# A decoder step whose instruction order is planned at build time: the plan's delays between engines raised, its 40 random rounds replaced by 1405 recorded steps

## The chip, the cores and the metric

The kernel runs on one core of one Trainium2 chip. The metric is the device time of one execution in microseconds, as the median of several runs. The profile is of one further execution.

The engines are TensorE (PE, matmuls; its weight loads are shown as PEld), VectorE (DVE), ScalarE (ACT), GpSimd (POOL) and SyncE (SP), which issues the DMAs. Each works through its own queue in the order in which its instructions were written, and waits on semaphores for what other engines have to deliver.

## The reference

One inference step of a two-layer decoder on 512 prompt tokens and 8 sequences of 8 sample tokens, all in float32, model width 1024:

```python
for i in range(DEPTH):                       # 2 layers
    h = rms_norm(x, norm_mix_pre[i])
    m = pool_mixer(h, ...) if i % 2 == 0 else gdn_mixer(h, ...)
    x = x + rms_norm(m, norm_mix_post[i])
    h = rms_norm(x, norm_ffn_pre[i])
    x = x + rms_norm(swiglu(h, ffn_w_in[i], ffn_w_out[i]), norm_ffn_post[i])
```

The pooling mixer takes trailing means over 2, 4, 8 and 16 positions and a small product per group of channels. The gated DeltaNet mixer projects to q, k, v, z and gates, runs a short causal convolution, normalizes q and k, and runs a chunked delta rule over 16 heads (a triangular inverse per chunk, then a recurrence over chunks that carries a state). A gate and an output product follow. Each SwiGLU FFN has an inner width of 2816. Outputs are the new tokens and all new states.

## The kernel before, in words

**Tiling.** The 576 tokens stand in the free dimension, in two halves of 256 and 320 columns (`HALVES`); channels stand in the 128 partitions. Products in float32 are made of three products of split operands: `mm3` (in `hybrid_kernel`) multiplies high by high, high by low and low by high parts. A weight tile is loaded as `wraw` (three buffers), rounded to `wh` on ACT, and the rest `wl` is made on DVE or POOL (`Weights.split`). The FFNs use a scheme with seven products in place of eight (`seven`). Results stand in eight PSUM banks, handed out in rings by `bank`: three for half one (`ps_A`), three for half two (`ps_B`), two for the mixer's projections (`ps_m`), two for the delta rule (`ps_k`), others for transposes (`ps_x`), the scan (`ps_s`) and norms (`ps_n`).

**Stages.** First the pooling mixer, then the FFN of layer 0, then the DeltaNet mixer in four groups of four heads, then the FFN of layer 1. In the mixer, `core` makes the delta rule of one group (`inv32`, `sample_front`, `scan`, `sample_heads`), `project` the projections of the next, `zproj` the z heads (`ps_m`, then Silu into `zz`, then out to memory), and `out0` the first half of the output product, kept in `y_d`. After the mixer its memory pools are closed; `yo` takes over their place, is loaded from `y_d`, and the second half of the output product is added to it.

**What sets the order.** The function does not issue instructions. Each call on an engine is recorded by `Plan.put` (reached through `Plan.Engine`) as an operation with its predecessors, its cost on each engine that may do it (`Plan.cost`: how long it holds the engine and when it is done), and the PSUM tiles it uses. There are 15384 such operations. `Plan.finish` then sets the order of all five queues:

- It gives each operation a rank, the length of the longest path from it to the end.
- `forward(rank)` plays the program through by the costs. At each moment, it takes the engine that is free first and gives it, of the operations that have become available, the one of the highest rank. An operation becomes available at the end of its last predecessor plus `LAT` of its own engine (between two PE operations, as soon as PE is free). Where PE would wait more than 300 ns, `idle_until` puts idle matmuls of `ones` into an unused bank (`ps_w`), which keep PE active. The model also follows PE's clock (`WINDOW`, `LOAD`) and the DMA queue. `forward` returns the order, the times and the whole length.
- `backward(order, times)` plays a given order from the end and returns the latest time for each operation; its negative is a new rank.
- In 40 rounds, the rank from `backward` is disturbed (`stirred`: all operations that write the same tile get the same random offset of up to 0, 300, 1000 or 3000 ns), `forward` is played again, and the shortest order is kept.

The order found is then issued, one instruction after the other (line 300; the idle matmuls on line 296).

Of the kernel before, what the change touches and what calls it, by code (L numbers as in the profile page):

```python
# [4 lines left out]

# [45 lines left out]
ZB = (0, 4, 8, 10, 12, 16)  # L51


class Plan:


# [208 lines left out]
    def finish(self):  # L267
        self.on = False
        ops = self.ops
        n = len(ops)  # L270
# [4 lines left out]
        rank = [0.0] * n
        for i in range(n - 1, -1, -1):
            e = ops[i][7]
            hold, done = ops[i][1][e]
# [4 lines left out]
            rank[i] = r
        draw = random.Random(self.SEED)
        here = best = self.forward(rank)
        for _ in range(self.ROUNDS):
# [4 lines left out]
            if found[0] < best[0]:
                best = found
        with self.tc.manual_schedule():
            for i, e in best[1]:
                if e is None:
                    self.tc.nc.tensor.matmul(self.banks[i[0]][i[1]][0][:, :self.idle.shape[1]], self.idle, self.idle,  # L296
                                             start=True, stop=True)
# [2 lines left out]
                calls[e](*a, **k)  # L300

    def stirred(self, rank, stir, draw):

        if not stir:
            return rank
        off = {}
        for o in self.ops:
            off.setdefault(self.name(o), stir * (2.0 * draw.random() - 1.0))
        return [r + off[self.name(o)] for r, o in zip(rank, self.ops)]
# [506 lines left out]

# [1131 lines left out]
```

## Time and profile before

| | us |
|---|---|
| median of 3 runs | 1572.15 (1570.51 to 1574.17) |
| the profiled execution | 1572.64 |
| its span, first to last instruction | 1570.9 |
| matmuls | 11962 |
| mean granted TensorE clock | 0.991 |
| bytes moved by DMA | 198.92 MB, mean 127 GB/s |

The profile gives, for each engine, the time in which it was busy, and, for each idle time, which instruction on which engine ended it. Nearly every instruction has line 300, the line that issues the plan, so groups are told apart by the names of their tiles: `ps_m<-hH,wh` is a matmul into a tile `ps_m` of the tiles `hH` and `wh`. Busy time by stretch, and of one tile alone, shows where in the kernel time is lost. The idle matmuls `ps_w` count as busy.

### The profile page before, as it was taken

How to read it: one execution, taken by the hardware profiler on the slowest of the kernel's cores; microseconds unless marked ns; L12 is line 12 of the kernel's file. 1: busy time of each engine (PE TensorE's matmuls, PEld its weight loads, DVE VectorE, ACT ScalarE, POOL GpSimd, SP SyncE). 2: the span in 40 equal slices, each digit the busy share in tenths (PEclk: the TensorE clock that was granted, in tenths of full speed). 3: DMA queues.
4: the chain of work that ended last, by engine and by line, in shares of the span. 5: the costliest groups of instructions: out<-in, count | busy, mean ns of one | idle time of the engine just before them, and what ended most of it. 6: DMA issues, size and time to landing. Idle time of an engine off the chain costs nothing. (4 is left out here: it accounts for less than half of the span.)

```text
span 1570.9 us, 30641 instructions
## 1 busy us (share of the span) xinstructions
PE 1542.9 (98%) x11962; PEld 1481.2 (94%) x11962; DVE 1154.5 (73%) x2333; ACT 841.1 (54%) x1756; POOL 113.1 (7%) x258
## 2 busy tenths in 40 slices
...
GB/s 184 103 178 142 82 94 95 96 80 91 151 210 158 83 119 117 102 123 100 136 109 108 106 127 120 201 140 179 248 173 177 107 81 73 88 110 68 98 187 119
DMA packets 350359, 198.92 MB, mean 127 GB/s; under 512 B 13963, under 2 KB 344364, under 8 KB 350207
## 3 DMA queue, kind: packets, MB, share of 16 engines
...
## 5 line engine op out<-in xcount | busy, mean ns | idle before, releaser
L300 ACT ACTIVATE wh<-wraw 128x1024 fp32r<-128x1024 f32 (+1 forms) x227 | 233.5, 1032 | 263.2 <-PE ps_B L300 94.4
L300 DVE TENSOR_TENSOR wl<-wraw,wh 128x1024 fp32r<-128x1024 f32 (+2 forms) x226 | 268.0, 1191 | 113.6 <-ACT wh L300 74.9
L300 PE MATMUL ps_m<-hH,wh 128*128 128x320 f32 (+1 forms) x832 | 244.1, 310 | 2.7 <-ACT zz L300 2.6
L300 PE MATMUL ps_m<-hL,wh 128*128 128x320 f32 (+1 forms) x832 | 242.4, 306 | 0.0
L300 PE MATMUL ps_m<-hH,wl 128*128 128x320 f32 (+1 forms) x832 | 239.2, 306 | 0.0
L300 PEld LDWEIGHTS ps_m<-hH,wh 128*128 128x128 f32 x832 | 153.3, 189 | 7.6 <-ACT zz L300 3.6
L300 PEld LDWEIGHTS ps_m<-hL,wh 128*128 128x128 f32 x832 | 154.0, 190 | 2.3 <-issue 0.6
L300 PEld LDWEIGHTS ps_m<-hH,wl 128*128 128x128 f32 x832 | 152.6, 190 | 2.8 <-issue 0.8
L300 PE MATMUL ps_B<-hH,wh 128*128 128x320 f32 (+1 forms) x392 | 115.8, 306 | 0.2
L300 PE MATMUL ps_B<-hH,wl 128*128 128x320 f32 (+1 forms) x392 | 115.0, 305 | 0.0
L300 PE MATMUL ps_B<-hL,wh 128*128 128x320 f32 (+1 forms) x392 | 114.6, 304 | 0.0
L300 PE MATMUL ps_A<-hH,wh 128*128 128x256 f32 (+1 forms) x376 | 106.0, 293 | 2.8 <-DVE yo L300 1.9
L300 PE MATMUL ps_A<-hH,wl 128*128 128x256 f32 (+1 forms) x376 | 105.6, 292 | 0.5 <-DVE wl L300 0.5
L300 PE MATMUL ps_A<-hL,wh 128*128 128x256 f32 (+1 forms) x376 | 104.5, 290 | 0.1
L300 PE MATMUL ps_B<-aH,wl 128*128 128x320 f32 x352 | 103.5, 312 | 0.2 <-DVE wl L300 0.2
L300 PE MATMUL ps_B<-aH,wh 128*128 128x320 f32 x352 | 102.4, 311 | 0.0
L300 PE MATMUL ps_B<-aL,wh 128*128 128x320 f32 x352 | 101.9, 310 | 0.0
L300 PE MATMUL ps_A<-aH,wh 128*128 128x256 f32 x352 | 95.1, 283 | 0.4 <-ACT wh L300 0.4
L300 PE MATMUL ps_A<-aL,wh 128*128 128x256 f32 x352 | 94.0, 281 | 0.0
L300 PE MATMUL ps_A<-aH,wl 128*128 128x256 f32 x352 | 92.9, 282 | 0.0
L300 DVE SCALAR_TENSOR_TENSOR ac<-u,cwt,ac 128x600 f32<-128x600 f32 x96 | 80.9, 850 | 1.9 <-ACT ac L300 1.7
L300 ACT ACTIVATE aH<-sg 128x576 fp32r<-128x576 f32 (+2 forms) x56 | 32.3, 581 | 84.7 <-DVE sg L300 84.7
...
## 6 DMA issues: line engine op xcount, KB each, us to landing
...
```

What stands on the lines that cost most here:

```text
L300: calls[e](*a, **k)
```

## The change

Only `Plan` is edited; the operations that are recorded stay the same.

1. The table of delays between engines, `LAT`, in ns by the engine that receives: PE from 55 to 190, ACT from 36 to 120, DVE from 36 to 120, POOL from 70 to 150; SP stays at 60.
2. The 40 random rounds go. In their place stand 1405 recorded moves, each a field "again.seed.stir.lo.hi" in base 36. For each move: if `again` is set (10 of them), the rank is replaced by the negative latest times of its own order; if `stir` is set (100, 300, 1000 or 3000 ns), the operations from `lo` to `hi` in the list get an offset of up to that size, from a hash of the seed and of the first operation that writes the same tile. Half of the moves span 400 operations or fewer. Moves lie in all parts of the list, most densely in its last quarter.
3. One last `forward` gives the order.

```diff
+MOVES = """
+1.1d7anak.0.rf.u7 1.y2f47l.2s.0.bvc 1.s0vq82.2s.0.ti 1.pp743b.0.0.bvc 1.4z4ke2.0.9qg.a1k 0.au7bb7.2s.7t9.bo5
...
-    LAT = {"PE": 55.0, "ACT": 36.0, "DVE": 36.0, "POOL": 70.0, "SP": 60.0}
+    LAT = {"PE": 190.0, "ACT": 120.0, "DVE": 120.0, "POOL": 150.0, "SP": 60.0}
...
-    ROUNDS, STIR, SEED = 40, (0.0, 0.0, 300.0, 1000.0, 3000.0), 2
...
-        draw = random.Random(self.SEED)
-        here = best = self.forward(rank)
-        for _ in range(self.ROUNDS):
-            late = self.backward(here[1], here[2])
-            found = self.forward(self.stirred([-t for t in late], draw.choice(self.STIR), draw))
-            if found[0] < here[0] or draw.random() < 0.1:
-                here = found
-            if found[0] < best[0]:
-                best = found
+        first = {}
+        of = [first.setdefault(self.name(o), i) for i, o in enumerate(ops)]
+        for move in MOVES.split():
+            again, seed, stir, lo, hi = (int(x, 36) for x in move.split("."))
+            if again:
+                rank = [-t for t in self.backward(*self.forward(rank)[1:])]
+            if stir:
+                for i in range(lo, hi):
+                    rank[i] += stir * self.noise(seed, of[i])
+        best = self.forward(rank)
...
+    @staticmethod
+    def noise(seed, who):
+
+        h = seed ^ (who * 2654435761 & 0xffffffff)
+        h ^= h >> 16
+        h = h * 0x85ebca6b & 0xffffffff
+        h ^= h >> 13
+        h = h * 0xc2b2ae35 & 0xffffffff
+        h ^= h >> 16
+        return h / 2147483648.0 - 1.0
```

More of the change, by code (lines that the diff above doesn't have):

```diff
@@ L2 @@
 import heapq
-import random
 from contextlib import ExitStack
@@ new lines @@
+0.xfacbh.2s.781.8dp 0.1fp5dk3.2bc.3ok.3zo 0.1slwoeh.2bc.70z.86n 0.1vgjcmy.2s.82h.985 0.1gi4m9f.2bc.4hm.4ke
+0.87h1q0.rs.54h.5fl 0.rfnq0w.8c.8ql.bvc 0.q4hmzs.8c.9sc.a3g 0.10nufsc.2s.0.1q5 0.1tiapdn.2s.b6l.bvc
+0.17t45od.rs.4a9.855 0.5rdedg.rs.9tc.9w4 0.1j4zh0k.2bc.6e.96 0.1ss67k0.rs.a6f.ahj 0.2svvgn.8c.agj.ajb
+0.bpoomp.rs.bpu.bsm 0.t3o181.2bc.41f.4cj 0.1wv9twd.2s.1ck.57g 0.1tf1mpa.8c.od.1u1 0.69rvzm.2bc.9fe.9qi
+0.1pj35r4.rs.9r8.9u0 0.1ce0uqr.8c.2um.40a 0.gjfyk0.8c.0.6p 0.46rblf.2s.3gc.3rg 0.14ty5f3.2s.8u9.9zx
@@ new lines @@
+0.g581av.8c.3cf.4i3 0.mnk81z.8c.8o2.8z6 0.qqg7s0.8c.8u9.9zx 0.1umehv5.8c.69r.6cj 0.163iv7o.8c.9zj.a2b
+0.1u5svau.rs.aa7.alb 0.gwwnl4.rs.3xw.490 0.8mc1r3.8c.6by.6eq 0.19w15z5.rs.9y7.a0z 0.ttisib.2bc.0.2w
+0.a7ikvn.2s.6mv.6pn 0.1bygjfd.2s.bnt.bvc 0.1koaur1.rs.8pn.90r 0.1wf7dro.rs.98t.9jx 0.ji5ev1.rs.a90.ak4
+0.1yp3jqj.rs.bfn.bif 0.1jv2yn6.rs.5vg.5y8 0.1mws14w.8c.8bp.9hd 0.i1evgw.2s.4gk.4jc 0.e2qeak.2bc.bb5.bm9
+0.11gd8un.rs.92n.95f 0.1favvlm.8c.1fj.1ib 1.3ktxmq.0.7cu.7fm 0.177ynii.rs.9pq.ave 0.1r5eqxe.8c.33t.3ex
@@ new lines @@
+0.ma35m2.rs.1d5.2it 0.lymuvx.8c.2td.34h 0.1x8yzja.2s.a8.454 0.muxcdo.8c.8sl.8vd 0.14uzngk.2s.5gn.6mb
+0.n0a1h5.8c.3t.3yp 0.1vmszuc.2s.36d.3hh 0.1kk9pm2.rs.7dk.7oo 0.17owqc0.2s.b0l.bvc 0.1cw9cxp.2bc.9n4.9y8
+0.elx6d7.8c.5in.6ob 0.1dkpzq2.2bc.86x.89p 0.9mpa4v.8c.5dp.5ot 0.jijbp0.2bc.b6h.bhl 0.x120r.2s.7cw.8ik
+0.2qokrq.rs.9ax.agl 0.ap74jx.rs.50w.5c0 0.1qf2ph5.rs.7w9.7z1 0.w56vte.rs.7ba.7e2 0.msgyjb.rs.6yq.84e
+0.psozk2.2bc.8p9.8s1 0.6ru0ma.2bc.aag.alk 0.1ilo347.2s.8nn.bvc 0.yqg8b1.2s.a62.a8u 0.1mz5fg.8c.9ek.ak8
@@ new lines @@
+0.7ta4rs.8c.5i9.5td 0.1a0iey2.rs.9wh.b25 0.m5lp1v.2s.38j.3jn 0.zowpr1.rs.241.2f5 0.18btd35.rs.9ha.amy
+0.67gkgs.8c.7lg.7wk 0.j1z5x4.2bc.98j.9jn 0.1p7860q.rs.91j.a77 0.1pz1vr6.rs.8mg.9s4 0.1fipxct.rs.973.9i7
+0.abp70g.rs.80m.8bq 0.15geaz8.2s.mv.pn 0.8n6wmv.rs.b8j.bvc 0.arqvcn.rs.1yx.21p 0.1osivhj.8c.3bg.3mk
+1.nd1zyp.rs.4lg.8gc 0.17z6qfn.2s.0.3g0 0.1renpzd.8c.9ja.aoy 0.10phdap.8c.81y.8d2 0.1s3qh7q.2bc.74c.774
+0.15e6smx.8c.1nb.2sz 0.1y1qmao.rs.5yz.61r 0.1qrour4.2s.0.31t 0.kdlkj4.2s.98f.9jj 0.du8s9v.8c.32y.3e2
@@ new lines @@
+0.zod3gs.rs.b1b.b43 0.kr24fj.rs.85t.8gx 0.jcsbb1.2s.7h9.8mx 0.1x13xnh.8c.1iq.1li 0.1ph2m2d.8c.jd.m5
+0.1obr04.2s.1bk.2h8 0.v8xpgw.2s.8ca.8f2 0.j1t9fl.8c.3g3.3r7 0.lmds8a.2s.bf2.bhu 0.mhzsom.2s.bhf.bvc
+0.g1j1ok.2s.893.9er 0.1ahwx7x.rs.80f.837 0.tj5xya.8c.akf.bq3 0.4n5glo.rs.9d2.9o6 0.15a5n8l.2s.7kq.7vu
+0.al1vf1.rs.97d.9ih 0.37vrb0.2bc.bfi.bia 0.30028l.2s.3wy.482 0.1t59vpp.8c.9ec.9h4 0.dlech0.2s.88d.8b5
+0.1v4x5fz.8c.6lg.7r4 0.1mwug70.rs.a1i.a4a 0.1ynuagv.2s.59y.5l2 0.12049ht.2bc.615.63x 0.t1q1ic.rs.9fy.alm
@@ new lines @@
+0.fxf9yv.rs.9eu.aki 0.1mgx6i9.2bc.55l.58d 0.vcvc52.8c.8zz.92r 0.19sl7ib.8c.7li.7wm 0.r0plbe.rs.asc.b3g
+0.7zanmx.rs.b05.bvc 0.12ufhff.8c.9jy.apm 0.4avjfd.8c.awb.b7f 0.hns5r3.rs.20o.23g 0.la7cq1.2s.9a9.afx
+0.7yxen0.2s.3xw.490 0.v5sum0.rs.arg.bvc 0.120epcx.2s.a48.afc 0.8u617z.8c.bu2.bvc 0.wteemh.8c.8am.8de
+0.wq6dw1.8c.b20.b4s 0.ez6f38.2s.bu1.bvc 0.12rv7la.2s.aob.btz 0.1ldfvg7.2s.bjn.bvc 0.169st4w.2s.3fz.4ln
+0.rvl2k.2s.88j.9e7 0.105hv1b.2s.jq.1pe 0.3i24yy.8c.brn.buf 0.f0oafc.2s.8oo.8zs 0.crohvn.8c.blc.bo4
@@ new lines @@
+0.1a6wowx.8c.211.36p 0.2vaufi.rs.72d.755 0.1skpskb.8c.1i3.1t7 0.10am2pk.rs.a9d.ac5 0.npr9rh.rs.24b.273
+0.133cb1c.2bc.7uc.7x4 0.zpf75r.8c.7y6.89a 0.1e0kerd.2s.8rp.8uh 0.y3nrgg.2s.147.29v 0.ic1sah.2s.6vj.817
+0.as0tuk.rs.998.9c0 0.wdwz0l.2s.74l.8a9 0.1hmua29.rs.on.rf 0.1ygkf9t.8c.6jb.6uf 0.td44m2.2bc.60u.76i
+0.4djklz.2s.8p1.8rt 0.i9dnnb.rs.ano.aqg 0.1a0nlzr.2bc.8gx.8jp 0.7e5kzs.rs.brq.bvc 0.cwbj70.rs.bn5.bpx
+0.9f65mp.8c.5sl.5vd 0.vaow4m.8c.8yd.99h 0.1vqw4gd.2s.lu.wy 0.kk5g02.rs.bub.bvc 0.os61rf.2s.5bn.6hb
@@ new lines @@
+0.14ymgs4.rs.7y.aq 0.15qc334.2bc.x8.18c 0.5xype4.rs.7qg.7t8 0.fsbcan.rs.aq2.asu 0.1isq969.2s.1kw.1no
+0.akw29y.8c.btb.bvc 0.983n1x.8c.392.3bu 0.zy6hgh.2bc.a2h.adl 0.15tdi24.2s.20.d4 0.qqm70d.2s.95b.9gf
+0.5deenj.2bc.32t.35l 0.gww8lj.8c.96c.ac0 0.zp4u65.rs.9e8.9pc 0.1bkp0wo.2bc.9un.9xf 0.e5frip.2s.9yj.a9n
+0.rbjxne.8c.90v.93n 0.lnwc6d.8c.a4j.afn 0.68ml7p.rs.81a.8ce 0.1whanj3.2s.9o4.9z8 0.1ap0evy.2s.8t6.94a
+0.846wh7.rs.9qi.aw6 0.m9x413.2bc.1rf.1u7 0.dnp293.2bc.vv.yn 0.1m4tbft.8c.1h.175 0.1avwtau.2s.9jv.9uz
@@ new lines @@
+0.1ferv49.rs.1q3.1sv 0.18dniux.2s.6dk.6oo 0.962bqv.2s.20r.2bv 0.1funypp.rs.23q.26i 0.krughu.2s.993.9k7
+0.1nh4ua8.2bc.5xc.604 0.9micho.2bc.1b9.1md 0.1luhrxo.rs.6gr.6rv 0.1e5dkj8.8c.but.bvc 0.72jtk0.8c.1j6.1ua
+0.1hajfzq.rs.b8s.bbk 0.c0iam7.8c.b6o.b9g 0.1yn8r7a.rs.ao6.aza 0.y4412n.8c.6vr.81f 0.aq7ncx.rs.68f.6jj
+0.vfb6oy.2s.9k3.apr 0.65hc7i.2s.ayn.b9r 0.1xbf449.8c.1zu.2ay 0.ftdhvo.2bc.bs2.buu 0.1c5lja1.2s.271.29t
+0.ee2zap.8c.awb.az3 0.1te02iy.2s.80i.966 0.1c7v44t.2s.3kl.3vp 0.1cuf56c.2bc.bfv.bin 0.gc9hkq.2bc.8en.8hf
@@ new lines @@
+0.owzpvt.2s.52m.5dq 0.7478ai.2s.ago.bvc 0.daqnqy.rs.bn9.bvc 0.5ewnzv.2s.6sn.73r 0.vf10t9.2s.b27.bdb
+0.uc4f9o.8c.9h3.9s7 0.1m6ldj7.2s.827.97v 0.1n987nh.8c.3rb.42f 0.13imgfq.2s.agg.aj8 0.16l2898.8c.40u.43m
+0.ipli2o.8c.79f.8f3 0.pved4z.2bc.832.85u 0.1cemryt.rs.56e.596 0.czf5e.8c.20b.35z 0.1vo1ezk.2bc.y2.10u
+0.1nz5gha.2s.b98.bvc 0.z3n245.8c.a44.a6w 0.1ol6btd.2s.6d5.7it 0.1e6dexg.8c.vb.20z 0.nb3yrk.8c.ane.ayi
+0.1xne3qg.rs.gj.rn 0.50b9w2.2bc.0.4y 0.1ebi93w.rs.1f4.1q8 0.16jmjwl.rs.7hv.7sz 0.1wekury.rs.9yv.a1n
@@ new lines @@
+0.p146o3.2s.a11.b6p 0.nifutj.2s.1cn.2ib 0.a0lg95.2bc.9id.9th 0.1mkohbn.rs.2ms.2xw 0.1e9t1b1.8c.ai5.at9
+0.11ehdyl.2s.2ng.2yk 0.qp739a.8c.1bx.1n1 0.1fnyuxg.rs.agb.arf 0.i3puxh.rs.3dh.3ol 0.wnek0a.rs.2l8.2o0
+0.12c45rx.8c.7og.7zk 0.p7l7xk.rs.2mk.2xo 0.m8svs3.8c.2jf.2uj 0.wwmkdk.8c.700.7b4 0.1fam1li.2s.3bl.4h9
+0.1ap8b8l.8c.5pj.6v7 0.11727m9.2s.387.4dv 0.w1nv7a.2s.221.2d5 0.19n6qt.8c.2is.2lk 0.v28qfw.8c.244.26w
+0.z5psjz.rs.178.1a0 0.u1tsaw.8c.3j7.3lz 0.4anz7x.2s.1at.2gh 0.165ml1r.2s.us.15w 0.5xdthc.8c.3ja.3m2
@@ new lines @@
+0.phlk0b.8c.anb.ayf 0.bkd3n0.2s.8j2.8u6 0.1ot43x2.2bc.ays.b1k 0.1ijdlv3.8c.29s.2ck 0.1cvizle.rs.4y1.50t
+0.y3jaqw.rs.4d8.4g0 0.jk6az6.2s.bg.mk 0.1xcck4u.rs.14y.17q 0.1pw4eap.rs.btx.bvc 0.ab4mf4.rs.98j.9bb
+0.1reo2j9.2bc.9ke.9n6 0.u4w7d8.2s.8h8.9mw 0.eqd0lz.8c.0.ek 0.1s41e77.8c.3c1.3et 0.j66va8.8c.aly.bvc
+0.1ffskko.8c.8xd.905 0.kb7rpo.2s.926.a7u 0.bec340.8c.8te.8w6 0.8h9c4r.2bc.bsb.bvc 0.168hxiq.rs.9h2.9s6
+0.uy0ir7.8c.24x.2g1 0.uu972d.2s.1f4.1q8 0.rscaiv.2s.1it.2oh 0.1h7cckq.rs.aje.aui 0.cwbk9k.rs.bpn.bsf
@@ new lines @@
+0.lpnbrj.8c.1dv.2jj 0.1k61jk1.rs.agm.aje 0.of059k.8c.45d.5b1 0.6xpjl8.2s.4lq.4oi 0.5r648o.8c.58a.5b2
+0.183zlwt.rs.5ex.5hp 0.1hnyyzv.rs.9ay.9m2 0.n3suf2.rs.7vc.7y4 0.1sm916b.8c.909.9bd 0.16q06a0.8c.9gt.9jl
+0.1fuxt3t.2s.3zj.557 0.1ewdmy9.rs.aol.azp 0.100aq7c.8c.2i.dm 0.1jbiu8c.2s.58a.5b2 0.mux4ia.2s.ac9.bhx
+0.2kg4pu.8c.apu.asm 0.78bakp.2s.523.5d7 0.ifhbna.2s.av2.b66 0.6o46dd.2s.3ki.4q6 0.h8gcpb.2s.9f3.9hv
+0.1phn9pe.8c.53v.5ez 0.1jb2m75.2s.40h.439 0.1k7ajny.rs.960.98s 0.1b17xqp.2s.4wh.4z9 0.vbu6ih.2s.9fd.9qh
@@ new lines @@
+0.1bbh00o.2s.0.1m7 0.7w1s60.rs.bpt.bvc 0.sk96g8.8c.34u.3fy 0.1m3msoc.8c.xh.18l 0.cvx7bo.rs.bog.bvc
+0.1lbj4lj.rs.boc.bvc 0.1f2kgc4.rs.ang.ayk 0.1ijflej.2s.4a2.5fq 0.mgf8yj.2bc.adh.aol 0.mdcc4c.8c.1d4.1fw
+0.1du75bo.rs.16n.1hr 0.xhlfm4.8c.axj.b8n 0.1xmccel.rs.b4q.b7i 0.b5tino.8c.3y7.49b 0.icyul4.8c.zb.24z
+0.1p9ez4y.rs.apu.asm 0.e5nryd.8c.aqv.atn 0.zo6o2c.2s.abr.bhf 0.1e9pdkk.2s.aph.b0l 0.1u2n0g2.8c.34d.375
+0.1jcjt2e.8c.59l.5cd 0.bw9zqy.rs.2yx.31p 0.ryl229.2bc.1yo.21g 0.1ljh2je.2s.aqn.atf 0.p07t8n.rs.an5.apx
```

216 lines of the change are left out of this document (209 added, 7 removed).

## The prediction

> **What bounds the kernel now.** I read the page first, then the busy time of each engine by stretch, then TensorE's waits, then the timeline at the two places where most of the loss sits.
>
> ```profile
> span 1570.9 us, 30641 instructions
> PE 1542.9 (98%) x11962; PEld 1481.2 (94%) x11962; DVE 1154.5 (73%) x2333; ACT 841.1 (54%) x1756; POOL 113.1 (7%) x258
> ```
>
> TensorE (PE) is busy for 1542.9 of 1570.9 us. Order can win only what PE loses, and 1570.9 - 1542.9 = 28.0 us of it is idle. The stretches are mine, cut at the two FFNs (89 to 430, 1186 to 1530). Columns: the stretch, its length, busy time and count for PE, PEld, DVE, ACT and POOL, the granted PE clock, the DMA share, GB/s.
>
> ```profile
> 0.00:89.00 89.00, 82.99 (x544) 77.14 (x545) 66.14 (x175) 57.74 (x131) 26.80 (x86) 0.88 0.52 149
> 89.00:430.00 341.00, 340.62 (x2540) 338.85 (x2540) 226.12 (x335) 142.71 (x216) 3.26 (x2) 1.00 0.38 109
> 430.00:1086.00 656.00, 643.20 (x5301) 594.10 (x5301) 528.21 (x1277) 419.77 (x1055) 71.61 (x158) 1.00 0.46 130
> 1086.00:1186.00 100.00, 97.20 (x752) 95.30 (x753) 75.20 (x160) 51.59 (x91) 10.81 (x12) 1.00 0.69 205
> 1186.00:1530.00 344.00, 343.97 (x2549) 342.86 (x2548) 235.43 (x349) 145.64 (x222) 0.61 (x1) 1.00 0.38 109
> 1530.00:1571.00 41.00, 34.93 (x284) 33.01 (x282) 23.36 (x40) 23.66 (x46) 0.00 (x0) 0.94 0.35 114
> ```
>
> Idle PE by stretch: head 6.0, first FFN 0.4, DeltaNet mixer 12.8, crossing to the second FFN 2.8, second FFN 0.0, end 6.1. The two FFNs, 685 us together, have nothing to give.
>
> Part of the busy time is no work. Where the plan foresees PE waiting over 0.3 us, it places idle matmuls into ps_w. The same stretches for that tile alone (PE and PEld):
>
> ```profile
> 0.00:89.00 89.00, 6.13 (x34) 5.41 (x34) 0.88 0.52 149
> 430.00:1086.00 656.00, 6.43 (x44) 5.57 (x44) 1.00 0.46 130
> 1086.00:1186.00 100.00, 9.57 (x80) 9.29 (x80) 1.00 0.69 205
> 1530.00:1571.00 41.00, 1.28 (x10) 1.20 (x10) 0.94 0.35 114
> ```
>
> That adds 6.1 + 6.4 + 9.6 + 1.3 = 23.4 us. Idle and filler together are 51.4 us, 3.3% of the span: the ceiling on any gain from order, apart from the clock.
>
> The waits inside the mixer are of another kind. TensorE's waits in 430 to 1086 (total us, times, longest); 18 groups, 28 waits, of which these are the first four and the last:
>
> ```profile
> PE ps_m L300 <- ACT zz L300: 2.6, 4, 1.0
> PE ps_x L300 <- DVE vt L300: 1.6, 4, 0.6
> PE ps_k L300 <- DVE ks L300: 1.5, 3, 0.6
> PE ps_x L300 <- DVE vs L530: 1.1, 2, 0.6
> ...
> PE ps_k L300 <- ACT wh L300: 0.2, 1, 0.2
> ```
>
> They are short, mostly 0.2 to 0.6 us, spread over the mixer, and most come after an answer of DVE or ACT. A wait that the plan had foreseen would hold fillers where it exceeds 0.3 us. These are mostly waits that it did not foresee: each answer came a little after the moment for which PE's next instruction had been placed.
>
> How long an answer really takes, on three rows (start, length, then the idle time before):
>
> ```profile
> 541.94 0.60 PE L300 MATMUL ps_x<-ident,qk 128*128 128x128 f32 x4
> ...
> 542.57 0.69 DVE L533 COPY u<-ps_x 128x512 f32<-128x512 f32 x1 [0.19 <-PE ps_x L300]
> ...
> 543.32 1.05 PE L300 MATMUL ps_x<-ones,sqs 128*128 128x1 f32 x8 [0.27 <-DVE u L533]
> ```
>
> PE ends at 542.54 and DVE starts at 542.57: 0.03 us. DVE ends at 543.26 and PE starts at 543.32: 0.06 us. The plan before counts 36 and 55 ns for these two answers, the plan after 120 and 190. So what errs in the old plan is not the answer's own delay but the durations on the way, and the new figures add a guard of 84 ns towards DVE and ACT and 135 ns towards PE: 0.219 us for each trip from PE to another engine and back.
>
> **The change part by part.** No operation is removed or added, apart from the number of fillers. Durations of real work therefore cancel, and the sum holds only PE's lost time. The order on all five queues can move, SP's DMA issues among them, since all are drawn from the same ranking.
>
> *The guard, in the mixer.* With it, the plan places about one or two products more (340.62 us / 2540 = 0.134 us each in the first FFN) ahead of a matmul that awaits an answer. What covers the wait is other PE work: the projections of the next group. 28 waits x 0.219 = 6.1 us if each is shortened by one trip's guard. Bounds: 0 if the cover is missing, 12.8 if nothing is left idle. Several trips often lie in a row, so I take 8, nearest to the 6.1 of the guard.
>
> *The recorded moves, in the mixer.* 1405 shifts of rank in place of 40 rounds. No row shows what they find; they can win the 6.4 us of fillers there at most, and at least nothing. I take the middle, 3.
>
> *The crossing.* Here most of the loss sits in one place:
>
> ```profile
> 1094.67 2.89 SPq L300 DMA_DIRECT2D wraw<-in_gdn_w_out_dram  x3
> 1094.72 6.86 PE L296 MATMUL ps_w<-ones 128*128 128x128 f32 x60
> ...
> 1097.66 6.54 SPq L300 DMA_DIRECT2D yo<-y_d  x11
> 1102.90 1.14 DVE L300 TENSOR_TENSOR yo<-yo,ps_A 128x256 f32<-128x256 f32 x3 [4.93 <-issue]
> 1103.47 0.36 PE L300 MATMUL ps_A<-hH,wh 128*128 128x256 f32 x1 [1.89 <-DVE yo L300]
> ```
>
> All three ps_A banks are full from about 1094.7. DVE frees them only when yo has been loaded from y_d. yo's first load is issued at 1097.66, because it takes over memory that the mixer holds until its last og has been split; it lands shortly before 1102.9. 6.86 + 1.89 = 8.75 us are lost, behind a DMA. SP's own figure in the plan does not change, so the guard does nothing here; another order could split the last og sooner or keep ps_B products (second half of the tokens) as cover. Bounds 0 and 8.75; I take 3, nearer to 0, since a transfer of 5 us stays. The crossing's other loss is 9.57 + 2.8 - 8.75 = 3.6 us; I take 1.
>
> *Head and end.* The head loses 6.0 + 6.1 us while the first tiles are loaded and normalized in one chain; I take 1 (bounds 0 and 5; the rest I count to the first data). PE's longest wait of all lies there, and then its last row at the end:
>
> ```profile
> PE ps_A L300 <- DVE xst L300: 2.1, 1, 2.1
> ```
>
> ```profile
> 1564.78 0.82 PE L300 MATMUL ps_B<-ident,gy 128*128 128x128 f32 x3
> ```
>
> PE is done at 1565.6, so 5.3 of the 6.1 us are the last scaling and storing, which no order covers. Of the other 0.8 + 1.3 us I take 1.
>
> *The FFNs.* 0: three banks for each ring and three weight buffers keep products ahead of PE, and 0.4 us of 685 is idle. What they hide is the splitting of each weight tile, two groups of the page:
>
> ```profile
> L300 ACT ACTIVATE wh<-wraw 128x1024 fp32r<-128x1024 f32 (+1 forms) x227 | 233.5, 1032 | 263.2 <-PE ps_B L300 94.4
> L300 DVE TENSOR_TENSOR wl<-wraw,wh 128x1024 fp32r<-128x1024 f32 (+2 forms) x226 | 268.0, 1191 | 113.6 <-ACT wh L300 74.9
> ```
>
> If the cover were gone, one tile would cost 1.03 + 1.19 = 2.2 us of PE's time; ACT, which waits 94.4 us for ps_B ahead of wh, shows how far in front it is.
>
> Sum: 8 + 3 + 3 + 1 + 1 + 1 = 17 us. The profiled execution took 1572.64 us, 1.7 us more than its span and 0.5 us above the median of the runs, 1572.15. 1572.64 - 17 = 1555.6, against the median 1555.2: I say **1556**.
>
> **The clock.** Four places show a reduced clock (PE's busy time follows the length):
>
> ```profile
> 6.00:20.00 14.00, 11.02 (x54) 10.33 (x53) 9.57 (x31) 10.14 (x23) 8.50 (x28) 0.64 0.87 237
> 54.00:58.00 4.00, 4.00 (x17) 3.64 (x16) 1.37 (x6) 1.44 (x4) 0.00 (x0) 0.57 0.72 222
> 81.00:89.00 8.00, 8.00 (x43) 8.00 (x43) 6.74 (x20) 0.52 (x2) 1.50 (x2) 0.57 0.77 230
> 474.00:478.00 4.00, 4.00 (x22) 3.94 (x21) 2.88 (x8) 0.69 (x2) 0.00 (x0) 0.57 0.39 103
> ```
>
> They cost (1 - 0.64) x 14 + 0.43 x 16 = 11.9 us of clock. Three of the four have PE fully busy. So here the clock falls without idleness, after few-column work such as the sums of squares. An order that thins out PE's work near a norm buys another such place at 0.43 x 4 = 1.7 us, one that packs it denser saves as much. I enter 0, with -5 to +5 for the range. The Trainium skill, page "TensorE: Matmul & The Clock Gate", section "HAM oscillation — how this bites in real kernels", gives the rule that PE should have no idle gap over about 3.4 us. By that rule the clock would be no matter of this change: the sum would be the same 17 and rival C below would have no chance. The rows at 54, 81 and 474 speak against it, since PE is busy throughout them and its longest wait is 2.1 us; so C keeps a chance.
>
> **The rivals.**
>
> *The waits are not of the order's making (A).* The losses that the plan already knows, 23.4 us of fillers, the 5.3 us end, the DMA at the crossing, stay because chains and transfers set them; the guard removes only a couple of microseconds of small waits and pays some back in other places. For it: 60 of the 168 fillers stand before one DMA. Against it: 12.8 us of unforeseen waits amid plenty of other PE work. Time: 1572.6 - 3 = 1570.
>
> *The guard slows the chain that sets the mixer's end (B), slower.* Each trip in the chain is served later, behind one more product. While a next group's projections remain, that is free. In the last group they run out: the cover is four z heads and half of the output projection, and at 1094.7 PE already has nothing left. Its scan makes 3 trips in each of 4 spans, the sample states and the block inverses about as many again: 25 x 0.219 = 5.5 us. It decides if PE has no free work at the chain's end, and if nothing else gains. Time: 1572.6 + 5.5 = 1578. Against it: PE idles only 12.8 us in 656, so chains seldom set the time now.
>
> *The clock (C).* Two or three more reduced places with no gain elsewhere: 1572.6 + 3 x 1.7 = 1578.
>
> *The record does not fit (D).* The noise depends on an operation's place in the list; if the list is not the one on which the moves were found, they are random shifts of up to 3 us. Idle and filler might double: 1572.6 + 51 = 1624. The diff leaves the list of operations alone, which speaks against it.
>
> **How the numbers follow.** Runs before spread over 0.23%, so 0.2%, 3 us, is about what can be told from no change: faster is below 1569, slower above 1575. My forecast (gains of 4 to 30 us) gets 0.78, A 0.10, B 0.07, C 0.04, D 0.01: faster 0.78, same 0.10, slower 0.12. The bounds sum to a gain of 12.8 + 6.4 + 8.75 + 3.6 + 5 + 2.1 = 38.7 (1534), which needs every term at its end; 30 is as far as I go below: 1543. Above, the range takes in A and the lower edge of no change: 1572. B, C, D and what exceeds 30 us make up about 0.2 outside.
>
> **What would show each step right or wrong.** Right: PE's waits in the mixer fall from 12.8 us to about 5, the rows on zz, vt and ks shrinking or gone; the fillers fall below 168; the yo wait at the crossing is shorter than 8.75 us; PE's busy time in the FFN stretches is unchanged. Wrong for the guard: the same number of waits in the mixer at the same length. B is seen if the mixer ends later than 1086 and fillers gather before it; C if more stretches show a clock near 0.57; D if PE's idle time rises everywhere. The forecast fails altogether if PE's idle and filler time stays near 51 us.

## The result, and the profile after

The kernel after takes 1529.95 us (median of 4 runs, 1528.16 to 1533.9); the kernel before took 1573.16 us beside it (4 runs, 1570.51 to 1575.55). The ratio is 0.9729, with a 95% interval of 0.9704 to 0.9755: 43.2 us are saved. The forecast, 1556.0 with a range of 1543 to 1572, had the direction and missed the size: 17 us were foreseen. The profiled execution after took 1528.16 us.

The page after, its span and the busy time of each engine:

```profile
span 1526.4 us, 30360 instructions
...
PE 1505.5 (99%) x11856; PEld 1454.6 (95%) x11856; DVE 1152.9 (76%) x2323; ACT 835.7 (55%) x1765; POOL 116.8 (8%) x259
```

PE's idle time is 1526.4 - 1505.5 = 20.9 us, 7.1 less than before. But its busy time fell by 37.4 us, and the prediction's sum had a place only for the fillers (the idle matmuls) in it, 12.9 us. The six stretches again, with their borders moved to where PE has done about as many real matmuls as at the borders of before; columns as there. The second fence is the idle matmuls (ps_w) alone, in the stretches that have any; at the crossing there is none.

```profile
0.00:82.00 82.00, 76.01 (x555) 70.66 (x556) 62.79 (x168) 56.79 (x131) 27.84 (x84) 0.98 0.54 151
82.00:420.00 338.00, 338.00 (x2535) 337.45 (x2534) 229.53 (x343) 143.37 (x216) 3.96 (x3) 1.00 0.38 111
420.00:1056.00 636.00, 627.40 (x5270) 585.04 (x5269) 527.18 (x1270) 418.23 (x1066) 71.67 (x159) 1.00 0.48 136
1056.00:1143.00 87.00, 87.00 (x677) 86.17 (x675) 73.07 (x156) 48.66 (x88) 11.41 (x12) 1.00 0.78 229
1143.00:1487.00 344.00, 343.36 (x2555) 342.98 (x2555) 237.39 (x350) 145.35 (x223) 1.94 (x1) 1.00 0.38 109
1487.00:1526.40 39.40, 33.74 (x276) 32.28 (x274) 22.89 (x40) 23.30 (x45) 0.00 (x0) 0.96 0.41 127
```

```profile
0.00:82.00 82.00, 7.56 (x42) 6.58 (x42) 0.98 0.54 151
420.00:1056.00 636.00, 1.93 (x12) 1.57 (x12) 1.00 0.48 136
1487.00:1526.40 39.40, 1.06 (x8) 0.97 (x8) 0.96 0.41 127
```

Set against the rows of before, each stretch falls into three parts: PE idle (length less busy), fillers, and PE busy with real matmuls (busy less fillers).

| stretch | foreseen, us | measured | idle | fillers | real matmuls |
|---|---|---|---|---|---|
| head | -1 | -7.0 | 0.0 | +1.4 | -8.4 |
| first FFN | 0 | -3.0 | -0.4 | 0 | -2.6 |
| mixer | -11 | -20.0 | -4.2 | -4.5 | -11.3 |
| crossing | -4 | -13.0 | -2.8 | -9.6 | -0.6 |
| second FFN | 0 | 0.0 | +0.6 | 0 | -0.6 |
| end | -1 | -1.6 | -0.4 | -0.2 | -1.0 |
| sum | -17 | -44.6 | -7.2 | -12.9 | -24.5 |

(The window of the end before reached 0.1 us past the span; the spans differ by 44.5. The borders agree to about six products, 0.8 us.) Read the mixer's row first: 5301 - 44 = 5257 real matmuls before and 5270 - 12 = 5258 after, the same work, and PE is busy with it for 643.20 - 6.43 = 636.8 us before and 627.40 - 1.93 = 625.5 us after. Over the whole span there are 11962 - 168 = 11794 real matmuls before and 11856 - 62 = 11794 after, and they fill 24.5 us less. So "busy" holds lost time that no row of PE's idle time shows.

One part of it is the clock. The four windows that the prediction listed, in the trace after:

```profile
6.00:20.00 14.00, 10.31 (x65) 8.92 (x63) 10.01 (x32) 10.40 (x24) 8.77 (x26) 0.88 0.99 284
54.00:58.00 4.00, 3.95 (x29) 3.61 (x28) 3.98 (x10) 3.46 (x9) 1.46 (x2) 1.00 0.25 85
81.00:89.00 8.00, 8.00 (x67) 7.84 (x66) 7.05 (x20) 4.64 (x8) 1.03 (x1) 1.00 0.65 192
474.00:478.00 4.00, 4.00 (x35) 4.00 (x35) 4.00 (x9) 2.13 (x6) 0.00 (x0) 1.00 1.00 263
```

The first has 0.88 in place of 0.64, the other three the full clock. What is lost there is 0.12 x 14 = 1.7 us in place of 11.9: 10.2 of the 24.5, 8.5 of it in the head, where real busy time is 8.4 less, and 1.7 in the mixer. That leaves about 14 us, some 10 of them in the mixer.

Most of this is short waits. A place where one can be watched is in the trace before, in the first FFN, a stretch that showed 0.4 us idle in all. Timeline from 111.35 (start, length, engine, instruction, in brackets the wait before it):

```profile
111.35 0.28 PE L300 MATMUL ps_A<-hL,wh 128*128 128x256 f32 x1
...
111.47 0.31 PE L300 MATMUL ps_B<-hH,wh 128*128 128x320 f32 x1
...
111.62 0.31 PE L300 MATMUL ps_B<-hL,wh 128*128 128x320 f32 x1
...
111.77 0.28 PE L300 MATMUL ps_A<-hH,wl 128*128 128x256 f32 x1
...
111.99 0.19 PEld L300 LDWEIGHTS ps_B<-hH,wl 128*128 128x128 f32 x1 [0.18 <-DVE wl L300]
111.99 0.41 PE L300 MATMUL ps_B<-hH,wl 128*128 128x320 f32 x1
...
112.25 0.30 PE L300 MATMUL ps_B<-hH,wh 128*128 128x320 f32 x1
```

A matmul's record lasts 0.28 to 0.31 us, but the next one starts 0.12 us later after 256 columns (111.35 to 111.47) and 0.15 us later after 320 (111.47 to 111.62): records overlap. The weight load at 111.99 waits 0.18 us for DVE's wl. The matmul at 111.77 has 0.22 us to itself in place of 0.12, and the one at 111.99 lasts 0.41 and has 0.26 in place of 0.15: 0.21 us late, and PE has no idle time at all. Only a wait that outlasts the record by itself, over about 0.28 - 0.12 = 0.16 us, begins to show on PE. The load (PEld) lasts 0.19 us at a spacing of 0.15 and shows all but 0.04 of the delay: 0.18 of 0.22 us (111.99 in place of 111.77). The Trainium skill, page "Perfetto Trace Analysis", section "Tensor Engine Instruction (MATMUL, LD_WEIGHTS)", says that a matmul's end in the profile is computed from its size and not observed. The overlap of these rows does not speak against it; no run here shows where a matmul really ends.

The loads also give the sum: PEld is off for 1570.9 - 1481.2 = 89.7 us before and 1526.4 - 1454.6 = 71.8 after, 17.9 less, where PE's idle time fell by 7.1. So 10.8 of the about 14 us are waits that the matmuls' records hide. The other 3 are not placed.

In the mixer the waits that do show fell from 12.8 to 8.6 us, not to about 5. Of the groups, the first two and the last of 10 (total us, times, longest):

```profile
PE ps_x L582 <- DVE vt L582: 3.0, 4, 2.0
PE ps_k L582 <- DVE ks L582: 0.9, 1, 0.9
...
PE ps_s L582 <- DVE vL L582: 0.3, 1, 0.3
```

The zz row, 2.6 us before, is gone, and 18 groups are 10; vt has grown from 1.6 to 3.0, with one wait of 2.0 us.

At the crossing nothing is lost any more: 87.00 of 87.00 us busy, no filler. SP's queue and DVE's first use of what it brings, and then DVE's last splits of og in the trace before:

```profile
1059.07 2.82 SPq L582 DMA_DIRECT2D yo<-y_d  x6
1063.26 0.38 SPq L582 DMA_DIRECT2D wraw<-in_gdn_w_out_dram  x1
```

```profile
1063.17 0.79 DVE L582 TENSOR_TENSOR yo<-yo,ps_A 128x256 f32<-128x256 f32 x2
```

```profile
1097.08 0.89 DVE L300 TENSOR_TENSOR hL<-og,hH 128x320 fp32r<-128x320 f32 x2
```

From yo's issue to its first use are 1063.17 - 1059.07 = 4.1 us, against 1102.90 - 1097.66 = 5.2 before. Before, DVE stood waiting for it; after, DVE came to it from other work without a wait, so 4.1 us is no more than an upper bound for the transfer. What changed is that it starts earlier against PE's work. Before, three loads of weights (2.89 us of issue) stood ahead of it in SP's queue, and SP had stood 4.5 us for DVE's wl, which frees the weight buffer, before it could issue the first of them; now single loads of weights stand between other things, and this one comes behind yo. The last splits of og were not what yo's first load waited for: it went out at 1097.66, while they ran until 1097.97.

### The profile page after: what moved, and what is told of

Read it like the earlier page. It is cut to its first block, busy times and chain, and to the rows that moved or that the text cites. A ratio compares the mean times of both kernels' runs of the same rounds, so it can differ in the third digit from the quotient of the medians.

```text
span 1526.4 us, 30360 instructions
## 1 busy us (share of the span) xinstructions
PE 1505.5 (99%) x11856; PEld 1454.6 (95%) x11856; DVE 1152.9 (76%) x2323; ACT 835.7 (55%) x1765; POOL 116.8 (8%) x259
## 5 line engine op out<-in xcount | busy, mean ns | idle before, releaser
L582 DVE TENSOR_TENSOR wl<-wraw,wh 128x1024 fp32r<-128x1024 f32 (+1 forms) x224 | 267.1, 1200 | 103.2 <-ACT wh L582 75.2
L582 PE MATMUL ps_m<-hH,wh 128*128 128x256 f32 (+1 forms) x832 | 246.4, 309 | 0.0
L582 PE MATMUL ps_m<-hL,wh 128*128 128x320 f32 (+1 forms) x832 | 246.4, 308 | 0.0
L582 PE MATMUL ps_m<-hH,wl 128*128 128x256 f32 (+1 forms) x832 | 244.9, 307 | 0.0
L582 PE MATMUL ps_B<-aH,wh 128*128 128x320 f32 x352 | 105.5, 311 | 0.6 <-ACT wh L582 0.6
L582 PEld LDWEIGHTS ps_B<-hH,wh 128*128 128x128 f32 x392 | 72.7, 188 | 0.1
```

## The experiments

**Theory G, the guard:** larger delays at the moment when an operation is placed leave room for an error that the plan does not know, and the gain lies in waits that come after the plan, many of them inside PE's busy time. **Rival S, the search:** the 1405 moves simply find a shorter plan, and the delays matter little. Besides, rivals B (a guard that slows chains), C (the clock) and D (moves that fit one list only) of the prediction. What tells G from S is a number that the program itself gives: the length of the plan that `forward` returns. Measured time less plan is what the plan did not foresee (it holds 1.7 us around the span). Larger delays also lengthen the plan by its own count, so a small difference alone is no gain; the measured time decides.

| kernel | delays | search | plan, us | measured | unforeseen |
|---|---|---|---|---|---|
| before | old | 40 rounds | 1530.3 | 1572.7 | 42 |
| old_40_s3 | old | 40, seed 3 | 1525.1 | 1569.0 | 44 |
| old_40_s4 | old | 40, seed 4 | 1526.7 | 1569.3 | 43 |
| guard_40 | new | 40 rounds | 1529.6 | 1551.7 | 22 |
| guard_40_s3 | new | 40, seed 3 | 1530.2 | 1551.4 | 21 |
| guard_40_s4 | new | 40, seed 4 | 1531.3 | 1548.2 | 17 |
| guard_small | a sixth of the guard | 40 rounds | 1523.2 | 1561.9 | 39 |
| guard_pe | new towards PE only | 40 rounds | 1528.3 | 1562.5 | 34 |
| guard_rest | new but towards PE | 40 rounds | 1536.6 | 1564.5 | 28 |
| crossing_only | old | 40 rounds, 49 moves | 1518.2 | 1565.0 | 47 |
| search_old | old | long, my own | 1498.8 | 1560.8 | 62 |
| search_mid | half the guard | long, my own | 1501.0 | 1533.4 | 32 |
| search_new | new | long, my own | 1502.8 | 1537.1 | 34 |
| search_dbl | twice the guard | long, my own | 1518.0 | 1538.7 | 21 |
| late_old | new, old in the last pass | the 1405 moves | 1517.9 | 1563.9 | 46 |
| after | new | the 1405 moves | 1499.9 | 1530.0 | 30 |
| longer_c2 | new | on from after's rank | 1496.3 | 1530.4 | 34 |
| longer_c3 | 240 / 150 / 180 | on from after's rank | 1507.0 | 1530.8 | 24 |

The kernels fall into four batches of four, in the order below (longer_c3 belongs to the last), and the kernel before was 1572.7, 1572.8, 1575.0 and 1572.3 us beside them. "My own" long search is one of the same kind: some 160,000 trial moves in the plan alone, of which those that shortened it were written down (178, 193, 154 and 184 moves, from search_old to search_dbl in the table).

**guard_40.** The new delays alone, on the kernel before.

```diff
-    LAT = {"PE": 55.0, "ACT": 36.0, "DVE": 36.0, "POOL": 70.0, "SP": 60.0}
+    LAT = {"PE": 190.0, "ACT": 120.0, "DVE": 120.0, "POOL": 150.0, "SP": 60.0}
```

> The kernel before with the later answers in LAT and nothing else: still 40 random rounds, no recorded moves. Two theories. Theory G (guard): the later answers shrink the time that the plan does not foresee. By its own count the plan of before is 1530.3 us long against 1572.6 us measured, 42 us unforeseen; the plan of after 1499.9 against 1528.2, 28 us unforeseen. This plan counts 1529.6 us, so G expects 1529.6 + 28 = 1558 us. Theory S (search): the long search alone makes the gain, the guard does nothing: about 1572 us, no change. If the guard only makes PE place real work later with no search to repair it: above 1575.

Measured 1551.71 us (1551.13 to 1554.11), ratio 0.9871 (0.9847 to 0.9895). The plan is 0.7 us shorter and the time 21 us: half of the whole gain without any better search.

**search_old.** A long search with the old delays: the kernel after with moves of my own, and

```diff
-    LAT = {"PE": 190.0, "ACT": 120.0, "DVE": 120.0, "POOL": 150.0, "SP": 60.0}
+    LAT = {"PE": 55.0, "ACT": 36.0, "DVE": 36.0, "POOL": 70.0, "SP": 60.0}
```

> A long search of its own (178 recorded moves out of about 160 thousand tried) with the true answers of before in LAT. By its own count the plan is 1498.8 us long, as short as that of after (1499.9). G expects 1498.8 + 42 = 1541 us: shorter than before by the search, but 13 us longer than after, with short unforeseen waits in the mixer. S expects the time of after, 1528 to 1531 us.

Measured 1560.83 us (1555.32 to 1573.92), ratio 0.9931 (0.9894 to 0.9968). The plan became 31.5 us shorter and the time 11.9: the search spends what slack the order had, and the unforeseen part grows from 42 to 62 us.

**search_new.** The same search with the new delays.

```diff
 MOVES = """
-1.1d7anak.0.rf.u7 1.y2f47l.2s.0.bvc 1.s0vq82.2s.0.ti 1.pp743b.0.0.bvc 1.4z4ke2.0.9qg.a1k 0.au7bb7.2s.7t9.bo5
...
+1.0.0.0.bvc 1.0.0.0.bvc 1.0.0.0.bvc 1.r2s5ow.2s.0.bvc 1.ojztdt.2s.0.bvc 0.ys794t.8c.43s.59g
...
```

> The same search with the same effort (154 moves), with the later answers of after in LAT; the plan counts 1502.8 us. Both theories expect about 1502.8 + 28 = 1531 us. It is the partner of the run with the true answers: their difference is the guard's share at equal search.

Measured 1537.12 us (1535.58 to 1538.32), ratio 0.9772 (0.9753 to 0.9792). Its plan is 4.0 us longer than search_old's and its time 23.7 us shorter. The pages of the two, first search_old, each with its fillers:

```profile
span 1560.4 us, 30448 instructions
...
PE 1526.9 (98%) x11866; PEld 1466.3 (94%) x11866; DVE 1154.5 (74%) x2319; ACT 836.4 (54%) x1767; POOL 119.1 (8%) x265
```

```profile
0.00:1600.00 1600.00, 12.08 (x72) 10.64 (x72) 0.99 0.43 124
```

```profile
span 1533.9 us, 30383 instructions
...
PE 1512.0 (99%) x11854; PEld 1458.7 (95%) x11854; DVE 1150.8 (75%) x2324; ACT 831.4 (54%) x1748; POOL 115.5 (8%) x263
```

```profile
0.00:1600.00 1600.00, 11.29 (x60) 9.50 (x60) 1.00 0.43 124
```

11794 real matmuls in both, busy for 1514.8 and 1500.7 us; idle 33.5 and 21.9; fillers alike. So the guard takes time from the visible waits and from the busy time, and almost none from what the plan foresees.

**crossing_only.** Old delays and old rounds, then 49 moves that touch only operations 9700 to 11700, around the crossing.

```diff
+        rank, first = list(kept), {}
+        of = [first.setdefault(self.name(o), i) for i, o in enumerate(ops)]
+        for move in MOVES.split():
+            _, seed, stir, lo, hi = (int(x, 36) for x in move.split("."))
+            for i in range(lo, hi):
+                rank[i] += stir * self.noise(seed, of[i])
+        best = self.forward(rank)
```

> The kernel before with its own LAT and its own best order, and 49 moves on its rank that touch operations 9700 to 11700 of the list alone, those around the crossing from the mixer to the second FFN. The plan counts 1518.2 us in place of 1530.3. If the crossing is what the prediction mis-sized, about 12 us go: 1560 us, the fillers near the crossing fall from 80 towards 10, and the wait on yo goes. If the loss there is set by the transfer, as the prediction took it, not more than 4 us go: 1568 us or more.

Measured 1565.02 us (1562.11 to 1567.47), ratio 0.9949 (0.9931 to 0.9968): 7.7 us. SP's queue, and the fillers around the crossing:

```profile
1090.08 3.83 SPq L322 DMA_DIRECT2D yo<-y_d  x4
1094.01 3.82 SPq L322 DMA_DIRECT2D wraw<-in_gdn_w_out_dram  x3
```

```profile
1040.00:1110.00 70.00, 1.72 (x14) 1.65 (x14) 1.00 0.58 168
```

The three loads of weights now stand behind yo, which starts 7.6 us earlier than before (1097.66), and ahead of the last two splits of og, which DVE begins at 1090.94. Of the 8.75 us lost there, 1.7 of fillers and a wait of 1.5 for yo are left. So the order of the DMA issues set most of this loss, and it goes without any guard. That this order did it alone is not shown: the 49 moves shift other operations around the crossing too. The time lies between the 1560 expected if the loss goes and the 1568 if the transfer sets it.

**old_40_s3, old_40_s4, guard_40_s3, guard_40_s4.** Is guard_40 a lucky draw? The kernel before and guard_40, each with two other seeds of the 40 rounds.

```diff
-    ROUNDS, STIR, SEED = 40, (0.0, 0.0, 300.0, 1000.0, 3000.0), 2
+    ROUNDS, STIR, SEED = 40, (0.0, 0.0, 300.0, 1000.0, 3000.0), 3
```

(and 4)

> The kernel before with the random seed 3 in place of 2; LAT and the 40 rounds as they were. The plan counts 1525.1 us, 5 us less than with seed 2. Theory G (the guard takes away time that the plan does not foresee): without the guard about 42 us are added, as in before: 1567 us. Theory L (the 21 us of guard_40 are the luck of one draw of an order): any place from 1550 to 1575 us, in the same band as the runs with the guard.

> The kernel before with the random seed 4. The plan counts 1526.7 us. G: 1526.7 + 42 = 1569 us. L: anywhere from 1550 to 1575 us.

> guard_40 with the random seed 3: the later answers, 40 rounds. The plan counts 1530.2 us, 5 us more than the same seed without the guard. G: 22 us are added as in guard_40, up to 28 as in after: 1552 to 1558 us, below its partner without the guard although its plan is longer. L: anywhere from 1550 to 1575 us.

> guard_40 with the random seed 4. The plan counts 1531.3 us. G: 1553 to 1559 us, below its partner without the guard. L: anywhere from 1550 to 1575 us.

Measured 1569.0 (1567.25 to 1571.32; ratio 0.9971, 0.9959 to 0.9983) and 1569.32 (1566.84 to 1583.49; 1.0006, 0.9978 to 1.0034) without the guard, 1551.43 (1548.88 to 1556.28; 0.9863, 0.9841 to 0.9884) and 1548.24 (1546.94 to 1549.72; 0.9839, 0.9824 to 0.9854) with it. Over three seeds the guard is worth 21.0, 17.6 and 21.1 us, with plans that are 0.7 us shorter and 5.1 and 4.6 us longer. The pages of seed 3, first without and then with the guard, and their fillers:

```profile
span 1565.5 us, 30579 instructions
...
PE 1533.0 (98%) x11924; PEld 1469.3 (94%) x11924; DVE 1154.7 (74%) x2332; ACT 843.8 (54%) x1767; POOL 112.9 (7%) x255
```

```profile
0.00:1600.00 1600.00, 20.08 (x130) 17.77 (x130) 1.00 0.43 124
```

```profile
span 1547.8 us, 30556 instructions
...
PE 1519.5 (98%) x11910; PEld 1465.2 (95%) x11910; DVE 1151.3 (74%) x2329; ACT 844.4 (55%) x1774; POOL 112.3 (7%) x250
```

```profile
0.00:1600.00 1600.00, 18.76 (x116) 16.50 (x116) 0.99 0.43 124
```

Real matmuls are busy for 1533.0 - 20.1 = 1512.9 us without and 1519.5 - 18.8 = 1500.7 us with the guard, though the guarded run had the lower clock over its span (0.994 against 0.997). Taking out the clock, (1 - clock) x span, gives 1508.2 and 1491.4. (For the kernel before that is 0.009 x 1570.9 = 14.1 us, 2 more than its four windows show.) The same sum for all profiled kernels that have a partner:

| kernel | idle | fillers | real matmuls busy | clock | real, clock taken out |
|---|---|---|---|---|---|
| before | 28.0 | 23.4 | 1519.5 | 0.991 | 1505.4 |
| old_40_s3 | 32.5 | 20.1 | 1512.9 | 0.997 | 1508.2 |
| old_40_s4 | 35.0 | 21.4 | 1509.0 | 0.998 | 1505.9 |
| search_old | 33.5 | 12.1 | 1514.8 | 0.994 | 1505.4 |
| late_old | 28.1 | 17.2 | 1517.7 | 0.997 | 1513.0 |
| guard_40 | 28.5 | 17.2 | 1503.7 | 0.995 | 1496.0 |
| guard_40_s3 | 28.3 | 18.8 | 1500.7 | 0.994 | 1491.4 |
| guard_40_s4 | 22.1 | 21.5 | 1501.6 | 0.993 | 1490.8 |
| search_new | 21.9 | 11.3 | 1500.7 | 0.996 | 1494.6 |
| after | 20.9 | 10.6 | 1495.0 | 0.998 | 1491.9 |

The last column parts these kernels by one thing alone: 1505 to 1513 where the last pass had the old delays, 1491 to 1496 where it had the new ones (0.8 us of each is the clock's rounding, and 1 to 2.4 us of each clock term lie behind PE's last matmul, where they cost nothing). The means, 1507.6 and 1492.9, lie 14.7 us apart: this is the guard's part inside PE's busy time. How much of it is hidden waiting, the loads tell: PEld's off time less PE's idle time falls with the guard by 4.7, 9.4 and 8.0 us in the three seeds, where the last column falls by 9.4, 16.8 and 15.1. About half is seen there; the rest is not placed.

The other profiled kernels, by the same sum: crossing_only, with the old delays, 1505.3; search_mid 1491.0, search_dbl 1491.3, longer_c2 1493.8 and longer_c3 1489.6; and, with a part of the guard, guard_rest 1498.0, guard_small 1496.6 and guard_pe 1494.6. So a part of the guard already has 9.6 to 13.0 of the 14.7 us.

**search_mid, search_dbl.** The long search with half and with twice the guard.

```diff
-    LAT = {"PE": 190.0, "ACT": 120.0, "DVE": 120.0, "POOL": 150.0, "SP": 60.0}
+    LAT = {"PE": 120.0, "ACT": 78.0, "DVE": 78.0, "POOL": 110.0, "SP": 60.0}
```

(doubled: PE 325, ACT and DVE 204, POOL 230)

> The same long search with half the guard: PE 120, ACT and DVE 78, POOL 110 ns (193 moves). The plan counts 1501.0 us. Without a guard the same search was 62 us longer on the chip than its plan (search_old), with the full one 34 us (search_new). If the guard works by its size: 1501 + 48 = 1549 us, half way between 1561 and 1537. If any guard that exceeds the true answer is enough: 1501 + 34 = 1535 us.

> The same long search with twice the guard: PE 325, ACT and DVE 204, POOL 230 ns (184 moves). The plan counts 1518.0 us, since it foresees waits that do not come. If a larger guard still takes away unforeseen time: 1518 + 15 = 1533 us; if the guard is used up at the size of after, about 1518 + 22 = 1540 us, longer than search_new although safer. Rival B of the prediction (the guard slows the chains) expects above 1545 us.

Measured 1533.38 us (1531.86 to 1534.12; 0.974, 0.9718 to 0.9762) and 1538.72 us (1537.11 to 1539.54; 0.9773, 0.9751 to 0.9796). Half a guard does as well as a whole one, two guards cost little: the unforeseen part falls on to 21 us, but the plan grows by 15.

**late_old.** The same moves, and so the same ranking, as the kernel after; only the last pass places by the old delays.

```diff
+        self.LAT = {"PE": 55.0, "ACT": 36.0, "DVE": 36.0, "POOL": 70.0, "SP": 60.0}
         best = self.forward(rank)
```

> The kernel after with one edit: the rank comes from the recorded moves as it is, but the last pass that makes the order from it uses the true answers. The plan counts 1517.9 us. If the gain lies in the rank that the moves found, most of it stays: 1530 to 1545 us. If it lies in the guard at the moment of placing, as theory G has it, the unforeseen time comes back: 1517.9 + 42 to 62 = 1560 to 1580 us.

Measured 1563.89 us (1561.98 to 1566.89), ratio 0.9936 (0.9911 to 0.9961). Page and fillers:

```profile
span 1563.0 us, 30410 instructions
...
PE 1534.9 (98%) x11894; PEld 1472.0 (94%) x11894; DVE 1155.3 (74%) x2328; ACT 831.1 (53%) x1760; POOL 111.1 (7%) x251
```

```profile
0.00:1600.00 1600.00, 17.20 (x100) 14.96 (x100) 1.00 0.43 124
```

With one ranking, 34 of the 43 us are lost again: 18 of them by the plan's own count, since the moves were found under the new delays, and 16 unforeseen. Against the kernel after, the real matmuls' busy time is 1517.7 - 1495.0 = 22.7 us longer.

**longer_c2, longer_c3.** Does a longer search go on winning? Some 190,000 more trials from the kernel after's rank, with its delays, and with slightly larger ones; the rank is written out as numbers.

```diff
-        for move in MOVES.split():
...
+        rank = [float(int(x, 36)) for x in RANK.split()]
```

> A further search from the rank of after, with the same later answers (190 thousand more trials, sideways steps allowed; the rank is written out as numbers). The plan counts 1496.3 us, 3.6 us less than that of after. If the 28 us that the plan does not foresee stay: 1525 us, a little below after at 1530. If the longer search also spends the guard: 1530 us or more.

> A further search from the rank of after with a larger guard: PE 240, ACT and DVE 150, POOL 180 ns. The plan counts 1507.0 us. The unforeseen time was 34 us at the guard of after with a long search and 21 us at twice the guard. Between them, 27 us: 1534 us, no better than after. If the larger guard reaches the 21 us: 1528 us.

Measured 1530.42 us (1527.99 to 1531.06; 0.9717, 0.969 to 0.9744) and 1530.76 us (1529.03 to 1532.26; 0.9729, 0.9707 to 0.9752). The first shortens the plan by 3.6 us and gains nothing; no run here beats the kernel after beyond the intervals.

**guard_pe, guard_rest, guard_small.** Which part of the guard works: the new delay towards PE alone, the new ones towards ACT, DVE and POOL alone, and about a sixth of all.

```diff
-    LAT = {"PE": 55.0, "ACT": 36.0, "DVE": 36.0, "POOL": 70.0, "SP": 60.0}
+    LAT = {"PE": 190.0, "ACT": 36.0, "DVE": 36.0, "POOL": 70.0, "SP": 60.0}
```

(guard_rest: 55, 120, 120, 150; guard_small: 80, 50, 50, 85)

> The kernel before, 40 rounds, seed 2, with the later answer towards PE alone (190 ns); ACT, DVE and POOL as before. The plan counts 1528.3 us. If the margin ahead of PE's own instructions is what helps: 1528.3 + 20 to 25 = 1548 to 1553 us, as guard_40. If only the sum over a trip counts: about 60% of the 20 us, 1560 us.

> The other half: later answers towards ACT, DVE and POOL (120, 120, 150 ns), 55 ns towards PE as before. The plan counts 1536.6 us, a poor draw. If the margin ahead of PE is what helps, the unforeseen 42 us stay: 1579 us. If the sum over a trip counts, about 40% of 20 us go: 1536.6 + 34 = 1571 us.

> The kernel before, 40 rounds, seed 2, with small excesses: PE 80, ACT and DVE 50, POOL 85 ns. The plan counts 1523.2 us. If any excess over the true answer is enough: 1523.2 + 22 = 1545 us. If the guard works by its size: 39 of 219 ns is a sixth, so 1523.2 + 39 = 1562 us.

Measured 1562.49 us (1559.46 to 1564.42; 0.9936, 0.9911 to 0.996), 1564.46 us (1562.84 to 1566.16; 0.9944, 0.9922 to 0.9966) and 1561.92 us (1560.18 to 1563.75; 0.9928, 0.9906 to 0.995). Unforeseen: 34, 28 and 39 us, against 42 without and 22 with the whole guard. Both directions count, as far as one draw of each can tell. For guard_small the two measures disagree. By the plan, 7.1 us are a shorter plan, a matter of the draw, and the unforeseen part fell by 3, where a sixth of 20 is 3.6. By the profile, idle time and fillers are as before (51.0 us against 51.4), and of the 12.4 us by which the span is shorter, 8.8 lie in the real matmuls without the clock and 3.2 in the clock. So whether the guard works by its size stays open.

## Why the prediction was right in direction and wrong in size

**The mechanism stands.** The old plan places PE's next instruction too soon after another engine's answer, and a guard of 84 and 135 ns covers that. That the new delays are a guard, and not better values for the answers, the trace before shows: where an engine had been idle for over 0.15 us, the median from the end of the answer to the start of the instruction that awaited it is 55 ns from DVE to PE (22 waits), 53 from ACT to PE (15), 37 from PE to ACT (262) and 38 from PE to DVE (119; the end of a matmul being the computed one), as in the old table. Which durations on the way the plan has wrong, no run here shows. Theory G holds: 17.6 to 21.1 us over three seeds, 23.7 at a long search, with plans that are hardly shorter or even longer. Rival S alone does not: at the old delays a search that shortens the plan by 31.5 us wins 11.9. But given the guard, search is worth 14.6 us (guard_40 to search_new) to 21.8 (guard_40 to after). The 43 us are about half and half.

**The step that failed first is the ceiling:** "Order can win only what PE loses, and 1570.9 - 1542.9 = 28.0 us of it is idle", with "Durations of real work therefore cancel". The real matmuls' busy time fell by 24.5 us: 10.2 by the clock, 10.8 by waits that lie inside overlapping records, and some 3 that are not placed. Idle time and fillers, the only lost time that the sum knew, fell by 20.1 against the 17 foreseen; but that is luck, since they came in another mix (crossing 12.4 for 4, mixer 8.7 for 11, head 1.4 more in place of 1 less). So the guard was sized by the wrong rows: 28 visible waits in the mixer gave 8 us, where a guard acts on every answer, visible or not, and was worth about 20 over the kernel. The row to read was PEld's. The Trainium skill, page "Perfetto Trace Analysis", section "Identifying the Most-Contended Engine", says that the matmuls' busy share is no good measure of TensorE's headroom and that the loads' share is a better one. The two pages of the profile agree: the loads' off time fell by 17.9 us, PE's own idle time by 7.1.

**The mixer's visible part** came out near its terms, in another mix: idle -4.2 where the guard was to bring -8, fillers -4.5 where the moves were to bring -3. That is 8.7 of the foreseen 11. The other 11.3 us of the stretch were busy time.

**The crossing:** "I take 3, nearer to 0, since a transfer of 5 us stays" failed: 12.4 us of idle time and fillers went. The transfer may have stayed (4.1 us at most), the wait did not. What set it was when yo was issued, and three loads of weights stood ahead of it in SP's queue: they end at 1094.67 + 2.89 = 1097.56, and yo goes out at 1097.66. The prediction quoted that row and still named the last split of og as the cause; that split was not yet done when yo went out. That "the guard does nothing here" is not contradicted: crossing_only wins 7.7 us with the old delays.

**The clock** was entered as 0 within 5 either way; it gave 10.2 between the two profiled executions. They lie near the ends of what the kernels show: ten executions of the kernel before beside guard_40 have 0.990 to 0.995, the four of the kernel after 0.996 to 0.998, and between their medians, 0.993 and 0.997, lie 0.004 x 1570 = about 6 us. That it is not the guard's doing the seeds show: profiled, the clock rises with the guard in seed 2 (0.991 to 0.995) and falls in seeds 3 and 4 (0.997 to 0.994, 0.998 to 0.993), and the gain is much the same. It differs from draw to draw of the order, and from execution to execution of one kernel, so 0 was a fair middle and 5 too narrow a bound.

**The FFNs, head and end:** 0 for the FFNs was wrong by 3 us in the first one (0.7 of it are five products fewer in the window) and about right in the second. Weight splits there do arrive 0.2 us late behind a PE that looks full, as at 111.99. Of the head's two terms, idle stayed at 6.0 and fillers grew by 1.4, so the 1 us foreseen for its order did not come; its 7 us are the clock. The end gave 1.6 for 1, of which 0.6 are idle time and fillers; the 1.0 of busy time are mostly six products fewer in the window.

**The rivals.** A would have kept the 23.4 us of fillers; 10.6 are left. B falls: the mixer ends at 1056, not after 1086, with 1.9 us of fillers, and with twice the guard the kernel still takes 1538.7 us. C came with the other sign. D falls with the kernel after itself; late_old shows that moves fit the delays under which they were found.

**The range** had 1543 as its lower end, from a gain of 30 us. Even the sum of all bounds, 38.7 us, gives 1534, and the kernel after lies below that: the bounds were all made from idle time and fillers. They left out the hidden waits, and the clock's bound was 5.

**Not settled:** why half the guard does as well as the whole at a long search (1533.4 against 1537.1; search_new and the kernel after, two searches at the same delays, differ by 7.2), and where in the kernel the guard saves most.
